# A hybrid decoder step with a dense expert stage: gate steps spread over the early up-projections, half of the expert selection one head later, the final norm by token blocks

## The chip, the core and the metric

The kernel runs on one core of a Trainium2 chip. The metric is the device time of one execution in microseconds, as the median of several runs; lower is better. The core has five engines with a queue of their own each: TensorE (PE, its weight loads are shown as PEld), VectorE (DVE), ScalarE (ACT), GpSimd (POOL) and SyncE (SP). An engine takes its queue strictly in order: an instruction that waits holds up all that stands behind it. Here SP only issues DMA transfers, and POOL almost only issues indirect DMAs, which gather rows from HBM by a list of numbers. All transfers share 16 DMA engines.

## What is computed

One inference step of one layer, for a prompt of 1024 tokens and 32 sample tokens (8 sequences of 4), at width 1024. The layer adds a token mixer (a gated delta rule and dilated windows), an attention to a memory of 256 entries, and PEER, a sparse expert layer; a last RMSNorm follows. The change is in PEER and in that norm, so these are the parts of the reference that matter:

```
def rmsnorm(x, g):
    xf = x.astype(F32)
    y = xf * lax.rsqrt(jnp.mean(xf * xf, axis=-1, keepdims=True) + NORM_EPS)
    return (y * g.astype(F32)).astype(x.dtype)

q = (xb @ w_pq).reshape(PEER_BLOCK, PEER_HEADS, 2, PEER_DHALF)      # 8 heads, two halves
s = jnp.einsum('thpc,hpnc->thpn', q, sub_keys)                      # 128 scores for each half
sv, si = lax.top_k(s, PEER_TOPK)                                    # best 16 of each half
cand = sv[:, :, 0, :, None] + sv[:, :, 1, None, :]
cv, ci = lax.top_k(cand.reshape(PEER_BLOCK, PEER_HEADS, 256), PEER_TOPK)
eid = i1 * PEER_NKEYS + i2                                          # i1, i2: taken from si by ci
gate = jax.nn.softmax(cv, axis=-1)
hid = jax.nn.gelu(jnp.einsum('thkd,td->thk', expert_u[eid], xb))
out = jnp.einsum('thk,thkd->td', gate * hid, expert_v[eid])
```

There are 16384 experts, and each token uses 8 heads x 16 = 128 of them.

## The kernel before

The prompt is cut into three groups of 384, 384 and 256 tokens (GROUPS); the 32 sample tokens go with the first (SG = 0, before and after the change). For each group `base` computes the mixer and the attention, and hands back `peer_route`, a generator that chooses the experts one head at a time. The chosen experts are then applied in one of two ways.

**By gathering** (`experts`, `experts_v`): 512 tokens of the first and third groups and the samples. For each of 128 slots POOL gathers the rows of expert_u that the tokens of a block want into a tile "gat" (128 x 1024, 4 buffers), DVE multiplies and sums them (L1282); after a GELU the same is done with expert_v, where DVE adds the row times its weight to the tile "acc" (L1431). That makes 1088 gathers of 512 KB. `paced` records them last of all, each behind an anchor instruction, and the scheduler that orders the finished program by its own estimates puts them wherever it finds room.

**Densely** (`dense`): the second group and the last 128 tokens of the third, 512 tokens (ND) together. All experts are computed for all tokens, in 128 slices of 128 experts, and a matrix of gates, zero almost everywhere, picks. Its parts, in the order of the program:

- The activations are loaded and split into a high and a low half ("C" and "B").
- 60 early up-projections (EARLY, chosen among the 128 slices): load a slice of expert_u ("wv", 2 buffers, L1347), split it on ACT and DVE ("wk", "zz"), 24 matmuls of 128x512, a GELU on ACT (L1355), and store the result to HBM (`uscr`, L1373). Between them stand the steps of `side`: the third group's `peer_route` (9 steps: one to begin, eight heads) and then `gate_extra`, 33 steps, of which 32 build the gates of four tokens each: DVE compares numbers (L1324, L1331), ACT does part of the comparing (L1330, L1333), four matmuls into "dl", and ACT copies the product into the halves "O" and "A" of the gate matrix (L1338). After each 8 of these steps SP stores both halves to `gscr` (L1341). PACE takes one step of `side` at every fourth early up-projection, 13 in all.
- What is left of `side` is run in one piece (`for _ in side`), then the tile "A" is taken again for the gates that are read back.
- The main loop, 128 slices (L1390 on): the gates of four slices are read back (`A<-gscr`, L1393), a slice of expert_v is loaded ("w", L1396) and split, the hidden values are multiplied by the gates (L1398), split, and multiplied by expert_v into eight sums in PSUM (tags "tp", "dl", "po", "ps"; the eighth goes through "vzs"). The 68 up-projections that were not early are computed between them.
- The eight sums are added to the residual "B" (L1423), and `finish_T` normalizes it: squares of all eight parts (L308), sums by matmul, a root on ACT (L321), a reciprocal, its spread over the partitions by matmul, eight multiplications (L328), then 32 transposes (L1467), eight copies (L1469) and eight stores (L1470).

`select` (called once or more for each head) takes the best 16 of the sums of both halves: DVE work on "tk" and "sel" that ends in the pair "ab" (L1242, L1243), a copy of the indices and one of "ab", spread 16-fold, on ACT (L1245, L1249, into "oh"), and DVE work that turns them into expert numbers (L1250 to L1256). In the first group it runs alone, in the second it is interleaved with `base` of the third group (`sprinkle`), and in the third with the early up-projections.

## Time and profile before

| | us |
|---|---|
| median of 3 runs | 4044.24 |
| these runs | 4036.69, 4044.24, 4068.52 |
| profiled execution, its own time | 4020.32 |
| its span, first to last instruction | 4018.5 |

| Stage, us of the span | what runs | TensorE busy | VectorE busy | DMA share |
|---|---|---|---|---|
| 772 to 905 | selection of the first group | 74% | 95% | 30% |
| 1530 to 2100 | base of the third group, selection of the second, gathers | 80% | 78% | 75% |
| 2394 to 2816 | early up-projections, selection of the third group, gathers | 98% | 86% | 95% |
| 2816 to 2889 | rest of the gate steps, gathers | 37% | 73% | 88% |
| 2889 to 3937 | main loop, gathers | 99% | 85% | 94% |
| 3937 to 3996 | end of the main loop | 100% | 51% | 31% |
| 3996 to 4018.5 | final norm and stores | 64% | 30% | 25% |

The profile is one execution; the sum of the prediction is made against its 4020.32 us, of which 1.8 us lie outside the span. It was 0.6% faster than the median of the runs shown. In its rows a line number is that of the kernel before, `out<-in` are the program's tile names, xN the number of instructions, and square brackets hold the idle time of the engine ahead of them and what ended it. The granted clock of TensorE (PEclk) is a share of 2.4 GHz.

### The profile page before, as it was taken

What the parts mean: (1) busy time and instruction counts of PE and PEld (TensorE: products, weight loads), DVE (VectorE), ACT (ScalarE), POOL (GpSimd) and SP (SyncE); (2) the same over time, 40 slices, a digit from 0 to 9 for tenths busy, and PEclk for the clock granted to TensorE, in tenths of its full rate; (3) what the DMA queues carried; (4) which work ended last, traced back from release to release, by engine and by line L of the source; (5) the groups of instructions that cost most, each with busy time, mean ns of one, the idle gap of its engine ahead of it and who ended that gap; (6) DMA issues with size and microseconds to landing.
All of it is one profiled execution on the core that took longest, in us unless ns stands there. A gap on an engine that the chain in (4) does not pass through costs nothing.

```text
span 4018.5 us, 53195 instructions
## 1 busy us (share of the span) xinstructions
PE 3533.0 (88%) x18135; PEld 2817.1 (70%) x18135; DVE 2889.7 (72%) x6660; ACT 1501.5 (37%) x3348; POOL 1358.8 (34%) x1255
## 2 busy tenths in 40 slices
PE   7998978968898787787887779999599999999999
PEld 6987865765676454456677657788477777787776
DVE  4334222599777766898669779997788888888885
ACT  5343413433233222123449652244533233333333
POOL 1000000001455554334333434444444444444441
PEclk9998878988999888887998889999799999999999
DMA  6443567423688888767768989999899999999994
GB/s 226 165 137 115 170 213 282 163 84 123 222 279 286 296 291 317 241 233 242 265 217 295 332 325 341 340 332 347 304 337 343 331 319 338 336 340 337 337 338 151
DMA packets 385600, 1074.23 MB, mean 267 GB/s; under 512 B 43280, under 2 KB 142160, under 8 KB 381232
## 3 DMA queue, kind: packets, MB, share of 16 engines
q0 software_dynamic: 159456, 580.58, 41.2%
q1 hardware_dynamic: 225872, 490.24, 34.9%
q8 instruction: 144, 2.36, 0.2%
q14 instruction: 128, 1.05, 0.1%
HBM read 995.22 MB, written 120.10 MB: 278 GB/s over the span
## 4 chain that ended last, share of the span: by engine, by line
PE 54%; DMA 13%; issue 12%; DVE 8%; POOL 7%; ACT 5%; POOLq 0%; SPq 0%; DVEq 0%; ACTq 0%
PE ps L150 36%; PE dl L150 10%; POOL gat L1273 7%; DMA gat<-expert_v,eid 5%; PE tp L150 4%; DMA gat<-expert_u,eid 3%; PE po L150 2%; DVE gat L1282 2%; DVE acc L1431 1%; ACT dtm L1330 1%; DMA w<-w_pq 1%; PE tp L870 1%; DMA zz<-ck 1%; DMA tmp<-tscr 0%; DVE dtm L1331 0%
## 5 line engine op out<-in xcount | busy, mean ns | idle before, releaser
L1273 POOL DMA_INDIRECT gat<-expert_u,eid x512 | 602.2, 1176 | 812.5 <-DVE hid L1282 482.4
L1273 POOL DMA_INDIRECT gat<-expert_v,eid x512 | 614.2, 1200 | 761.5 <-DVE acc L1431 566.0
L1431 DVE SCALAR_TENSOR_TENSOR acc<-gat,hid,acc 128x1024 f32<-128x1024 f32 x544 | 696.6, 1280 | 145.7 <-DMA gat<-expert_v,eid 138.6
L1282 DVE CUSTOM_DVE_ANT_0 gat<-gat,fr 128x1024 f32<-128x1024 f32 x544 | 660.0, 1219 | 137.2 <-DMA gat<-expert_u,eid 131.3
L150 PE MATMUL dl<-dtm,dtm 128*128 128x128 f32 (+2 forms) x2400 | 334.4, 290 | 62.0 <-ACT C L1338 20.6
L150 PEld LDWEIGHTS dl<-dtm,dtm 128*128 128x128 f32 (+1 forms) x2400 | 310.8, 203 | 84.4 <-ACT C L1338 23.5
L150 PE MATMUL ps<-C,w 128*128 128x384 f32 x768 | 283.6, 529 | 42.4 <-DMA w<-w_pq 32.3
L150 PE MATMUL dl<-O,dtm 128*128 128x512 f32 x1152 | 306.3, 396 | 0.0
L1291 ACT ACTIVATE dtm<-w 128x512 fp32r<-128x512 f32 x288 | 177.9, 628 | 300.7 <-PE dl L150 213.4
L150 PE MATMUL ps<-C,wk 128*128 128x512 f32 x1024 | 266.2, 402 | 24.8 <-ACT C L1291 17.0
L150 PE MATMUL ps<-C,zz 128*128 128x512 f32 (+1 forms) x1088 | 277.5, 391 | 0.0
L1291 ACT ACTIVATE wk<-wv 128x1024 fp32r<-128x1024 f32 x128 | 135.8, 1061 | 358.6 <-PE ps L150 304.8
L150 PEld LDWEIGHTS ps<-C,w 128*128 128x128 f32 x768 | 156.9, 209 | 151.0 <-DMA w<-w_pq 33.9
L150 PE MATMUL ps<-B,wk 128*128 128x512 f32 x1024 | 262.3, 398 | 0.0
L150 PEld LDWEIGHTS dl<-O,dtm 128*128 128x128 f32 x1152 | 217.2, 189 | 52.6
L150 PE MATMUL tp<-O,dtm 128*128 128x512 f32 x768 | 220.8, 403 | 31.3 <-ACT O L1291 30.5
L150 PEld LDWEIGHTS ps<-C,wk 128*128 128x128 f32 x1024 | 192.4, 191 | 74.9 <-ACT C L1291 18.9
L1292 DVE TENSOR_TENSOR dtm<-w,dtm 128x512 fp32r<-128x512 f32 x288 | 196.6, 685 | 66.1 <-issue 28.8
L150 PEld LDWEIGHTS ps<-C,zz 128*128 128x128 f32 x1088 | 204.3, 188 | 45.5
L150 PEld LDWEIGHTS ps<-B,wk 128*128 128x128 f32 x1024 | 194.4, 190 | 45.9
L150 PE MATMUL ps<-O,dtm 128*128 128x512 f32 x768 | 224.2, 396 | 0.0
L1292 DVE TENSOR_TENSOR zz<-wv,wk 128x1024 fp32r<-128x1024 f32 x128 | 156.5, 1223 | 74.2 <-ACT wk L1291 70.9
(500 smaller groups left out, 6346.4 us busy)
## 6 DMA issues: line engine op xcount, KB each, us to landing
wv<-expert_uT SPq DMA_DIRECT2D x128, 512.0 KB
w<-expert_v SPq DMA_DIRECT2D x128, 512.0 KB
w<-w_in SPq DMA_DIRECT2D x102, 512.0 KB
s_win<-cache_win SPq DMA_DIRECT2D x64, 512.0 KB
A<-gscr SPq DMA_DIRECT2D x32, 1024.0 KB
w<-w_pq SPq DMA_DIRECT2D x48, 512.0 KB
gscr<-C SPq DMA_DIRECT2D x12, 2048.0 KB
uscr<-tmp SPq DMA_DIRECT2D x60, 256.0 KB
```

Of the source, the lines that this page charges most:

```text
L150: x = self.nc.tensor.matmul(out, lhsT, rhs, **kw)
L870: nc.tensor.transpose(tp[:r, c, :], es[hh][:lq, j, o:o + r], C["ident"][:lq, :lq])
L1273: return self.nc.gpsimd.indirect_dma_start(out=dst, out_offset=None, in_=src, in_offset=bass.IndirectOffsetOnAxis(ap=idx, axis=0))
L1282: nc.vector.tensor_tensor_reduce(out=u, in0=u, in1=fr, scale=1.0, scalar=0.0, op0=ALU.mult, op1=ALU.add, accum_out=hid[:, s:s + 1])
L1291: nc.scalar.activation(hi, x, AF.Copy)
L1292: nc.vector.tensor_tensor(lo, x, hi.bitcast(F32), op=ALU.subtract)
L1330: nc.scalar.activation(o2[:, j], self.CB["iota"], AF.Abs, bias=i2[:, t:t + 1], scale=-1.0)
L1431: nc.vector.scalar_tensor_tensor(acc, v, c[:, s:s + 1], acc, op0=ALU.mult, op1=ALU.add)
```

## The change

There are four edits; SG and the groups are as before.

1. PACE is replaced by CLOSE and OPEN. The 41 steps of `side` are spread evenly over the first 50 early up-projections, the last stores follow at the 50th, and at the 56th the tile "A" is taken again and the first gates are read back (`load_gates(0)`). Nothing of `side` is left behind the early up-projections.
2. `select` becomes a generator in two halves. The second half, from the ACT copies on, is run a head later, after that head's top 16. "ab" gets a tag of its own ("sab", 3 buffers), "sel" has 5 buffers in place of 8.
3. `finish_T` works on blocks of 128 tokens: eight transposes into two PSUM tiles ("tp", "dl"), squares with their sum straight from PSUM on ACT, one addition, root and reciprocal, and two multiplications by root and gain straight from PSUM on DVE, each followed by its store. The gain is loaded as a row, spread over the partitions ("gf", in a "w" buffer).
4. `dense` returns the gain with the residual.

```
-PACE = (1, 1, 1, 1, 1, 1, 1, 1, 1, 1, 1, 1, 1)
+CLOSE, OPEN = 50, 56
@@ sel
-        return self.t(shape, "sel", 8, dt)
+        return self.t(shape, "sel", 5, dt)
@@ peer_route
+        late = []
         for h in range(8):
...
+            for x in late:
+                next(x, None)
+            late = []
             for b in range(0, nb, 2):
                 bs = slice(b, min(b + 2, nb))
-                self.select(P, sv[:, bs], si[:, bs], eid[:, h, bs], gate[:, bs, h])
+                late.append(self.select(P, sv[:, bs], si[:, bs], eid[:, h, bs], gate[:, bs, h]))
...
+            for x in late:
+                next(x)
+        for x in late:
+            next(x, None)
@@ select
-        ab = self.sel((P, 2, 2, 16), I32)[:m, :nb]
+        ab = self.t((P, 2, 2, 16), "sab", 3, I32)[:m, :nb]
         nc.vector.tensor_scalar(ab[:, :, 0], f, 4, None, op0=ALU.logical_shift_right)
         nc.vector.tensor_scalar(ab[:, :, 1], f, 15, None, op0=ALU.bitwise_and)
+        yield
         sf = self.sel((P, 2, 2, 16), BF16)[:m, :nb]
@@ dense
+        def load_gates(e):
+            nc.sync.dma_start(gs[e // GI % 2].rearrange("p s i t -> p s (i t)"),
+                              self.gscr[:, :, e * UT:(e + GI) * UT].rearrange("s p u -> p s u"))
+
         early = {e: i for i, e in enumerate(e for e in range(P) if e * EARLY // P != (e + 1) * EARLY // P)}
+        steps = 9 + EX // 4
         for e, i in early.items():
-            for _ in range(PACE[i // 4] if i % 4 == 0 and i // 4 < len(PACE) else 0):
-                next(side, None)
+            for _ in range((i + 1) * steps // CLOSE - i * steps // CLOSE if i < CLOSE else 0):
+                next(side)
+            if i == CLOSE:
+                for _ in side:
+                    pass
+            if i == OPEN:
+                gs = self.t((P, 2, ND // UT, GI, UT), "A", 1)
+                gs = [gs[:, j] for j in range(2)]
+                load_gates(0)
             nc.sync.dma_start(self.uscr[i], self.expert_up(e, fh, fl))
-        for _ in side:
-            pass
         self.rate = RATES[3]
-        gs = self.t((P, 2, ND // UT, GI, UT), "A", 1)
-        gs = [gs[:, j] for j in range(2)]
...
         h = self.t((P, KD, ND), "B", 1)
         nc.sync.dma_start(h, self.tscr[1])
+        gf = self.t((P, D), "w", WB)
+        nc.sync.dma_start(gf, I["g_final"].to_broadcast([P, D]))
@@ finish_T
-        self.norm_T(self.ks(h), 4, ND, self.ks(h))
-        for b in range(L // P):
-            self.rows(h, b * P, P, self.O["y_p"], t0 + b * P)
-        if EX:
-            self.rows(h, N1, EX, self.O["y_p"], SEQ - EX)
+        parts = [(c0, P, O["y_p"][t0 + c0:t0 + c0 + P]) for c0 in range(0, L, P)]
+        parts.append((N1, EX, O["y_p"][SEQ - EX:]))
+        for c0, m, out in parts:
+            qs = [self.p((P, 4, P), tag) for tag in ("tp", "dl")]
+            ss, y = self.small((P, 2)), [self.tmp() for _ in range(2)]
+            for i, q in enumerate(qs):
+                for k in range(4):
+                    nc.tensor.transpose(q[:m, k], h[:, 4 * i + k, c0:c0 + m], C["ident"])
+                nc.scalar.activation(y[i][:m], q[:m], AF.Square, accum_out=ss[:m, i:i + 1])
+            r = self.small((P, 1))
+            nc.vector.tensor_tensor(r[:m], ss[:m, :1], ss[:m, 1:], op=ALU.add)
+            nc.scalar.activation(r[:m], r[:m], AF.Sqrt, scale=1.0 / D, bias=C["eps"][:m, :1])
+            nc.vector.reciprocal(r[:m], r[:m])
+            for i, q in enumerate(qs):
+                z = y[i].rearrange("p a b -> p (a b)")
+                nc.vector.scalar_tensor_tensor(z[:m], q[:m].rearrange("p a b -> p (a b)"), r[:m], gf[:m, i * 512:(i + 1) * 512], op0=ALU.mult, op1=ALU.mult)
+                nc.sync.dma_start(out[:, i * 512:(i + 1) * 512], z[:m])
```

What this does to the order of the finished program is shown at three places. The first is TensorE among the early up-projections. An up-projection is three rows ("wk" twice, "zz" once); a head of the third group's selection is the four rows with "w" (w_pq) and "sk". Before, from one head on:

```order
L150 MATMUL ps_17561<-A_11016,w_17552 128x256 x8
L150 MATMUL ps_17571<-sk_17556,tmp_17560 128x128 x2
L150 MATMUL ps_17589<-A_11016,w_17554 128x256 x8
L150 MATMUL ps_17599<-sk_17556,tmp_17588 128x128 x2
L150 MATMUL ps_17660<-C_16428,wk_17656 128x512 x8
L150 MATMUL ps_17660<-B_16427,wk_17656 128x512 x8
L150 MATMUL ps_17660<-C_16428,zz_17657 128x512 x8
L150 MATMUL ps_17694<-C_16428,wk_17690 128x512 x8
```

Now, from one head on:

```order
L150 MATMUL ps_17107<-A_11016,w_17098 128x256 x8
L150 MATMUL ps_17117<-sk_17102,tmp_17106 128x128 x2
L150 MATMUL ps_17135<-A_11016,w_17100 128x256 x8
L150 MATMUL ps_17145<-sk_17102,tmp_17134 128x128 x2
L150 MATMUL ps_17206<-C_16428,wk_17202 128x512 x8
L150 MATMUL ps_17206<-B_16427,wk_17202 128x512 x8
L150 MATMUL ps_17206<-C_16428,zz_17203 128x512 x8
L150 MATMUL ps_17243<-A_11016,w_17234 128x256 x8
```

Before, three more up-projections followed before the next head; now the next head follows after one. All eight heads lie within nine up-projections, where they took up 32.

The second place is SP around the stores of the gates. The "A" that is read back is the one that the main loop needs first. Before, from the second pair of stores on:

```order
L1341 DMA gscr<-O_19489 128x2048
L1341 DMA gscr<-A_19490 128x2048
L1341 DMA gscr<-O_19629 128x2048
L1341 DMA gscr<-A_19630 128x2048
L1396 DMA w_20130<-expert_v 128x1024
L1341 DMA gscr<-O_19769 128x2048
L1341 DMA gscr<-A_19770 128x2048
L1396 DMA w_20175<-expert_v 128x1024
L1393 DMA A_19909<-gscr 128x16x128 x2
```

Now, from the last pair of stores on:

```order
L1350 DMA gscr<-O_19123 128x2048
L1350 DMA gscr<-A_19124 128x2048
L1356 DMA wv_19637<-expert_uT 128x1024
L1413 DMA w_20175<-expert_v 128x1024
L1395 DMA uscr<-tmp_19564 128x512
L1356 DMA wv_19671<-expert_uT 128x1024
L1395 DMA uscr<-tmp_19600 128x512
L1380 DMA A_19773<-gscr 128x16x128 x2
L1395 DMA uscr<-tmp_19634 128x512
```

The loads and stores of up-projections stand between the last stores of gates and their reading; before, the stores of three parts and the reading stood nearly side by side, behind all early up-projections.

The third place is DVE at the end of the main loop, from the next-to-last split of expert_v on ("dtm"), up to the additions to "B". Before:

```order
L1292 TENSOR_TENSOR dtm_27142<-w_27136,dtm_27141 128x512
L1419 TENSOR_TENSOR vzs_16429<-vzs_16429,ps_27077 128x512
L1292 TENSOR_TENSOR O_19910<-tmp_27069,O_19910 128x512
L1292 TENSOR_TENSOR dtm_27146<-w_27136,dtm_27145 128x512
L1292 TENSOR_TENSOR O_19910<-tmp_27113,O_19910 128x512
L1423 TENSOR_TENSOR B_27178<-B_27178,tp_19911 128x512
```

Now:

```order
L1301 TENSOR_TENSOR dtm_27142<-w_27136,dtm_27141 128x512
L1450 SCALAR_TENSOR_TENSOR acc_29867<-gat_30625,hid_29869,acc_29867 128x1024
L1436 TENSOR_TENSOR vzs_16429<-vzs_16429,ps_27077 128x512
L1301 TENSOR_TENSOR O_19911<-tmp_27069,O_19911 128x512
L1301 TENSOR_TENSOR dtm_27146<-w_27136,dtm_27145 128x512
L1450 SCALAR_TENSOR_TENSOR acc_29867<-gat_30628,hid_29869,acc_29867 128x1024
L1415 TENSOR_TENSOR tmp_27113<-tmp_27113,A_19773 128x512
L1450 SCALAR_TENSOR_TENSOR acc_29867<-gat_30631,hid_29869,acc_29867 128x1024
L1301 TENSOR_TENSOR O_19911<-tmp_27113,O_19911 128x512
L1450 SCALAR_TENSOR_TENSOR acc_29867<-gat_30634,hid_29869,acc_29867 128x1024
L1450 SCALAR_TENSOR_TENSOR acc_29867<-gat_30637,hid_29869,acc_29867 128x1024
L1442 TENSOR_TENSOR B_27178<-B_27178,tp_19912 128x512
```

The sums over gathered rows now go on up to the additions: 23 of them stand behind the last split of an up-projection ("zz"), where 2 stood before. Over the whole program their number is the same, 1088; from the first to the 63rd split of an up-projection there are 190 of them where there were 188, the piece of gate steps behind it, which held 32, is gone, and the main loop holds them as densely as before, about six for each up-projection.

## Rows read from the trace of the kernel before

**Rows 1.** Stretches: length, busy PE, PEld, DVE, ACT, POOL (instructions), clock, DMA share, GB/s
```profile
2394.00:2889.00 495.00, 440.14 (x2019) 362.38 (x2019) 416.90 (x1046) 203.23 (x374) 219.27 (x188) 0.95 0.94 337
...
2816.00:2889.00 73.00, 26.73 (x168) 25.14 (x168) 53.36 (x102) 44.75 (x113) 26.65 (x23) 0.69 0.88 309
...
3937.00:3996.00 59.00, 58.94 (x256) 46.16 (x254) 29.94 (x44) 19.84 (x31) 2.27 (x3) 1.00 0.31 116
```

**Rows 2.** Timeline of TensorE, rest of the gate steps: start, duration, [idle <-releaser]
```profile
2808.54 1.05 PE L150 MATMUL dl<-dtm,dtm 128*128 128x128 f32 x8
...
2855.13 7.42 PE L150 MATMUL dl<-dtm,dtm 128*128 128x128 f32 x40 [7.76 <-ACT A L1338]
2889.38 1.22 PE L150 MATMUL tp<-O,dtm 128*128 128x512 f32 x2 [26.83 <-ACT O L1291]
```

**Rows 3.** Timeline of SP there: last stores of gates, first reading
```profile
2864.54 0.64 SPq L1341 DMA_DIRECT2D gscr<-A  x1
...
2877.30 5.35 SPq L1393 DMA_DIRECT2D A<-gscr  x2
```

**Rows 4.** Waits, 2806 to 2900: us in total, times, longest
```profile
PE tp L150 <- ACT O L1291: 26.8, 1, 26.8
...
PE dl L150 <- ACT A L1338: 18.7, 5, 7.8
```

**Rows 5.** Stretches: four up-projections and a head; up-projections alone
```profile
2480.00:2511.50 31.50, 30.56 (x136) 24.84 (x136) 29.26 (x93) 9.15 (x14) 13.73 (x13) 1.00 0.94 346
...
2700.00:2740.00 40.00, 40.00 (x176) 32.54 (x175) 29.82 (x47) 12.88 (x17) 22.85 (x20) 1.00 0.99 362
```

**Rows 6.** The same stretch, L1282 on DVE alone
```profile
2480.00:2511.50 31.50, 14.66 (x24) 1.00 0.94 346
```

**Rows 7.** Groups, 2394 to 2890: busy us, mean ns | idle before <-releasers
```profile
L1292 DVE TENSOR_TENSOR zz<-wv,wk 128x1024 fp32r<-128x1024 f32 x61 | 74.6, 1223 | 23.5 <-ACT wk L1291 23.4
...
L1291 ACT ACTIVATE wk<-wv 128x1024 fp32r<-128x1024 f32 x61 | 64.7, 1060 | 162.7 <-PE ps L150 113.9 <-DMA wv<-expert_uT 26.3 <-DVE hid L1282 7.2
...
L1330 ACT ACTIVATE dtm<-cb,i 128x128 f32<-128x128 bf16 x96 | 30.0, 397 | 0.0
L1338 ACT ACTIVATE A<-dl 128x256 f32<-128x256 f32 x32 | 20.0, 666 | 0.0
L1338 ACT ACTIVATE O<-dl 128x256 f32<-128x256 f32 x32 | 19.1, 640 | 4.8 <-PE dl L150 4.8
L1333 ACT ACTIVATE dtm<-dtm 128x512 f32<-128x512 f32 x24 | 14.6, 634 | 0.0
```

**Rows 8.** Stretches, the gathers on POOL alone (xN)
```profile
2889.00:3937.00 1048.00, 474.47 (x391) 1.00 0.94 334
3937.00:3996.00 59.00, 1.15 (x1) 1.00 0.31 116
```

**Rows 9.** The spread copy of the selection on ACT: idle before it, who waited
```profile
  DVE sel L1243: 104.3, 28
...
  DVE oh L1250: 8.9, 8
```

**Rows 10.** Stretch: the first group's selection
```profile
772.00:905.00 133.00, 98.24 (x519) 85.27 (x518) 125.69 (x738) 48.99 (x107) 4.62 (x5) 0.91 0.30 98
```

**Rows 11.** Timeline, the final norm
```profile
3996.53 0.68 DVE L1423 TENSOR_TENSOR B<-B,ps 128x512 f32<-128x512 f32 x1
...
4000.19 1.28 ACT L321 ACT_TABLE_LOAD   x1
...
4001.49 0.26 ACT L321 ACTIVATE small<-ps,cf 128x4 f32<-128x4 f32 x1
4001.79 0.18 DVE L322 RECIPROCAL small<-small 128x4 f32<-128x4 f32 x1 [4.58 <-ACT small L321]
...
4003.28 5.35 DVE L328 SCALAR_TENSOR_TENSOR B<-B,gains,ps 128x512 f32<-128x512 f32 x8 [1.31 <-PE ps L150]
...
4014.78 0.60 ACT L1469 ACTIVATE tmp<-ps 128x512 f32<-128x512 f32 x1 [0.35 <-PE ps L1467]
```

More of the change, by code (lines that the diff above doesn't have):

```diff
@@ L1213, in peer_route @@
                 self.store_rows(hres, gi, self.hscr)
+            for x in late:
+                next(x, None)
+            late = []
             for b in range(0, nb, 2):
                 bs = slice(b, min(b + 2, nb))
-                self.select(P, sv[:, bs], si[:, bs], eid[:, h, bs], gate[:, bs, h])
+                late.append(self.select(P, sv[:, bs], si[:, bs], eid[:, h, bs], gate[:, bs, h]))
             if gi == SG:
-                self.select(NS, sv[:NS, nb:nb + 1], si[:NS, nb:nb + 1], eid[:NS, h, nb:nb + 1], gate[:NS, nb:nb + 1, h])
+                late.append(self.select(NS, sv[:NS, nb:nb + 1], si[:NS, nb:nb + 1], eid[:NS, h, nb:nb + 1], gate[:NS, nb:nb + 1, h]))
+            for x in late:
+                next(x)
+        for x in late:
+            next(x, None)
         for b, (m, c0) in enumerate(blocks):
@@ L1390, in dense @@
         for e in range(P):
-            if e % GI == 0:
-                g = gs[e // GI % 2]
-                nc.sync.dma_start(g.rearrange("p s i t -> p s (i t)"),
-                                  self.gscr[:, :, e * UT:(e + GI) * UT].rearrange("s p u -> p s u"))
+            g = gs[e // GI % 2]
+            if e % GI == 0 and e:
+                load_gates(e)
             v = self.t((P, KD, P), "w", WB)
@@ L1445, in finish, with finish_T @@
         nc.gpsimd.dma_start(out, acc)
-    def finish_T(self, h):
+    def finish_T(self, h, gf):
+        nc, C, O = self.nc, self.C, self.O
         t0, L = GROUPS[1]
-        self.norm_T(self.ks(h), 4, ND, self.ks(h))
-        for b in range(L // P):
-            self.rows(h, b * P, P, self.O["y_p"], t0 + b * P)
-        if EX:
-            self.rows(h, N1, EX, self.O["y_p"], SEQ - EX)
+        parts = [(c0, P, O["y_p"][t0 + c0:t0 + c0 + P]) for c0 in range(0, L, P)]
[15 more added lines that the diff above has]
+                nc.sync.dma_start(out[:, i * 512:(i + 1) * 512], z[:m])
     def store_rows(self, src, gi, scr):
@@ L1592, in run @@
                 self.sprinkle(1000)
-                self.finish_T(self.dense(route))
+                self.finish_T(*self.dense(route))
                 break
```

2 lines of the change are left out of this document (1 added, 1 removed).

## The prediction

> **What bounds the kernel now.** I read the stretches first. Ahead of the main loop TensorE is busy for 440.1 of 495 us, and its idle time is nearly all in one piece: from 2816 to 2889 it works 26.7 of 73 us, at a granted clock of 0.69 (that is the lower of its levels, 1.2 GHz, for much of the stretch; it had waited before) [rows 1]. The timeline shows why. This is the rest of the gate steps, which come after the last early up-projection: TensorE waits for ACT's copies between short bursts (7.76 us before the last), and then 26.83 us for the first operand of the main loop [rows 2]. That last wait is made on SP's queue: the last store of gates is issued at 2864.54 and the first reading of gates, which must see it landed, at 2877.30 [rows 3]; the rest is the reading itself. The waits of the stretch say the same: 26.8 us for ACT's "O", 18.7 us for the copies [rows 4]. In the main loop no such gap is left: its gathers run at 2.68 us each (1048 us / 391) with the DMA engines at 334 GB/s, and they end 59 us before the loop does; in these 59 us one gather is issued and the DMA rate is 116 GB/s [rows 1, 8]. So TensorE sets the end, with the gathers a reserve of some 59 us behind it.
>
> **Term 1, the gate steps among the early up-projections.** Removed: TensorE's idle 495 - 440.1 = 54.9 us, and the low clock. The 168 gate matmul records of the gap took 26.7 us; at the full-clock row, 1.05 us for 8 [rows 2], they would take 22.0. The floor ahead of the main loop is then 440.1 - 4.7 = 435.4 us, and 59.6 us can be gained at most.
>
> Against that stands what now lies in one place. By the order, the eight heads lie in nine up-projections, and DVE has there 9 splits, 49 gathered rows and 278 of the 378 selection instructions. Prices: a split is 1.22 us [rows 7]; a gathered row is 14.66 / 12 = 1.22 us [rows 6]; a head is what is left of a stretch of four up-projections and one head, 29.26 - 14.66 - 4 x 1.22 = 9.7 us [rows 5, 6]. DVE: 9 x 1.22 + 49 x 1.22 + 278/378 x 8 x 9.7 = 128 us. TensorE: an up-projection is 24 of the 176 records of a stretch that holds little else, 40 x 24 / 176 = 5.45 us, and a head 30.56 - 4 x 5.45 = 8.8 us [rows 5], so 9 x 5.45 + 8 x 8.8 = 119 us. DVE is thus longer by 9 us, and TensorE, which needs each split, waits for it. If DVE keeps the idle time that it has now (31.5 - 29.26 = 2.2 us for each head), it is 27 us. I take 10, nearer the lower end, because DVE has work queued from several sources there.
>
> Next, 19 of the 32 gate steps lie in seven up-projections. On ACT a step is (30.0 + 20.0 + 19.1 + 14.6) / 32 = 2.6 us [rows 7], and an up-projection 1.06 for the split and 0.63 for the GELU, at the price of L1333's shape [rows 7]: 19 x 2.6 + 7 x 1.69 = 61 us, against TensorE's 7 x 5.45 + 19 x 1.05 = 58. That costs 3 us. The halves "O" and "A" have one buffer each, so a part's first copy waits until the last part's store has landed, up to 12.8 us [rows 3], with the up-projections' ACT work queued behind it. Of the three such places two have several up-projections between, and one has about one; I take 2 us, bounds 0 and 38. On SP the wait before reading the gates back now has five issues of up-projections ahead of it; behind it stand up-projection loads that are two slices early. I cost it at nothing; without that cover it is 12.8 us. All of it: 59.6 - 10 - 3 - 2, about **-45 us** (-60 to 0).
>
> Do the transfers fit? The 495 us move 337 x 0.495 = 167 MB. Of these 30 gathers of 0.524 MB leave (32 of the gap go, the rest has 2 more), so 151 MB are left for 435 to 450 us, 336 to 347 GB/s. A 40 us stretch at 362 GB/s had TensorE busy all through [rows 5]. It fits, with little to spare.
>
> **Term 2, the second half of the selection a head later.** ACT's spread copies wait 104.3 us for DVE, 28 times, and hold up what stands behind them [rows 9]. In the first group this gives little: DVE is busy for 125.7 of 133 us [rows 10], so at most 7.3 us. The second group's selection runs within the base of the third, where no engine is near full and the trace does not show how much of a wait reaches the end; I allow the same again. DVE's 8.9 us of waiting for these copies [rows 9] may grow. I take **-3 us**, bounds -15 and +60 (the upper one is a rival below).
>
> **Term 3, the final norm.** Now: 21.3 us from the last addition's end (3997.2) to the end of the span (4018.5), and 3.1 of these behind the last copy [rows 11]. By blocks: the last four transposes, at the price of four gate matmuls, 1.05 [rows 2]; a square of the same shape as the copy, 0.60; root and reciprocal, 0.26 and 0.18, an addition like the latter; two multiplications of 5.35 / 8 = 0.67 [rows 11]. That is 3.6, with handovers 4.5 us for the first block. Of the later ones TensorE needs 2.1 each and waits for freed PSUM tiles, so 2.5: 4.5 + 7.5 + 3.1 = 15.1. **-6 us**, bounds -10 and 0.
>
> On ACT the new order has 71 table loads where it had 68. In the trace a load takes 1.28 us and the root follows 1.30 us after its start [rows 11], so three more are 3.9 us of an engine that does not set the end; I count nothing. The Trainium skill (ScalarE: Activation LUTs, "What ACT_TABLE_LOAD costs") gives 1.28 us and a drain of 1.38 on top for a switch. By it the three would be 8 us, and the sum, were all of them on the path, 8 us higher; the row here shows the load without the drain.
>
> **Term 4, the gathers at the end.** 21 more rows now stand behind the last up-projection's split. In 59 us that is 2.8 us each, against 2.68 in the loop, and 21 x 0.524 + 116 x 0.059 = 17.9 MB, 303 GB/s, below the loop's 334 [rows 1, 8]. But the additions to "B" now stand behind the last gathered row on DVE, and the squares behind the square of "acc" and a table load on ACT. **+2 us**, bounds 0 and +8.
>
> **Sum.** -45 - 3 - 6 + 2 = -52, from 4020.3 to 3968.3 us for an execution like the profiled one. The median shown is 4044.24 / 4020.32 = 1.006 times that execution; so I forecast **3992 us**.
>
> **Rivals.** *DVE bounds the packed heads.* The 27 us above in place of 10: -35 in sum, 3985, as a median 4009. For it: DVE is at 93% there now [rows 5]. Against it: its gathered rows are only loosely placed.
>
> *The transfers bound the packed stretch.* If it runs only at the 309 GB/s of the present gap [rows 1], where gate stores and gathers mix as they now will, 151 MB take 489 us and 6 of the 59.6 us are left: -13 in sum, 4007, as a median 4031. Against it: 362 GB/s was reached, and in the gap DVE and ACT held the gathers back.
>
> *DVE waits for ACT in turn (slower).* The late copy stands in ACT's queue behind work of the base that waits for TensorE, and DVE behind the copy. If each of the second group's 16 selections costs DVE the 3.7 us that ACT waits now (104.3 / 28), that is 60 us: +8 in sum, 4028, as a median 4053. It decides from 3.3 us each on, and is slower by over 1% from 5.8. Against it: that wait is now 8.9 / 8 = 1.1 us.
>
> *All covers hold.* DVE and ACT overlap as their sums allow and the first two selections give 15: -59.6 - 15 - 8 = -83, 3938, as a median 3961.
>
> **Chances.** The forecast 0.52 (its own range 3972 to 4010), DVE 0.18, transfers 0.12, the reversed wait 0.06, all covers 0.12. For the range I reach to the best case's 3961 with a little room, and above to the transfers' 4031: 3955 to 4040. One per cent, about what a measurement of this kernel can tell from no change, is 40 us: faster means under 4004. That holds for the best case, for most of the forecast (0.45) and a quarter of the DVE case: 0.62. Slower by over 1% needs the reversed wait at its worst, or a cost that I don't see: 0.05. The rest, 0.33, is the same.
>
> **What would show it.** Between the last early up-projection and the main loop TensorE's gap is gone and its clock stays at 1.0; from the start of the early up-projections to the main loop's first matmul it is about 450 us in place of 495. In the packed heads DVE is near 100% and TensorE shows short waits for splits. ACT's wait for L1243's successor is gone from the first two selections, with DVE's wait for the copy still small. The gathers' last issue lies within 10 us of the loop's end. From the last addition to the end there are about 15 us. I am wrong if the early part is not shorter than 475 us, if the main loop's TensorE falls under 98% because gathers come late, or if the base of the third group gets longer.

## The result, and the profile after

The changed kernel takes 3998.3 us (median of 4 runs, 3989.8 to 4007.5) against 4041.7 us (4 runs, 4036.7 to 4068.5, one more than those shown ahead): a ratio of 0.988, interval 0.983 to 0.993, a gain of 43 us. The gain is clear of none; whether it is more than one per cent the interval leaves open. Measured once more beside the experiments it is 0.9885 (0.9857 to 0.9913), 39 us between the medians.

One thing must be known before the traces are compared. The profiled execution of before took 4020.3 us, 21 us less than the median of its runs; that of after took 3995.9, 2 us less than its own. The two traces are thus only 24.4 us apart (4018.5 and 3994.1), and so I compare stretch by stretch. The stretches of the changed kernel (columns as in [rows 1]; the last two rows of this fence are the main loop and the end behind its last multiplication):

```profile
2405.33:2864.03 458.70, 438.01 (x2019) 360.07 (x2020) 386.70 (x1026) 202.11 (x372) 213.25 (x168) 0.98 0.94 339
2430.00:2590.00 160.00, 146.75 (x646) 119.00 (x645) 149.75 (x540) 41.47 (x68) 70.81 (x59) 0.98 0.89 314
2590.00:2790.00 200.00, 200.00 (x999) 167.65 (x998) 171.43 (x366) 132.44 (x267) 96.91 (x74) 1.00 0.96 349
2790.00:2864.00 74.00, 68.01 (x281) 54.45 (x280) 43.55 (x37) 19.72 (x24) 32.14 (x24) 0.95 0.98 352
2864.03:3978.04 1114.01, 1098.84 (x4659) 871.60 (x4658) 940.53 (x1224) 349.65 (x529) 504.41 (x421) 1.00 0.94 330
3978.04:3994.10 16.06, 5.46 (x32) 4.32 (x30) 10.43 (x23) 6.10 (x20) 0.56 (x1) 0.66 0.43 163
```

The early part, from the first store of an early result to the main loop's first matmul, is 458.7 us long where it was 495 [rows 1]. The gap ahead of the main loop is gone: from 2590 to 2790 us, where most gate steps now lie, TensorE is busy all the time at a granted clock of 1.00. The main loop takes 1114.0 us in place of 1106.0 (its last matmul ended at 3995.4 us before), and the end 16.1 in place of 23.1. That is -36.3 + 8.0 - 7.0 = -35.3 us. The dense part starts 11 us later than in the trace of before (2405.3 and 2394.4), which leaves some 24; whether the change did that is a question for the experiments.

What is left of TensorE's idle time in the early part (waits: us in total, times, longest; the third row ends as the stretch begins):

```profile
PE ps L150 <- ACT tmp L1204: 14.7, 16, 3.9
PE ps L150 <- ACT wk L1300: 6.0, 2, 4.4
PE ps L150 <- ACT tmp L1364: 5.1, 1, 5.1
```

14.7 + 6.0 is all of 458.7 - 438.0 = 20.7 us. L1204 is ACT's copy of a query of a head. In the packed heads it is late for a reason that the timeline shows (start, duration, [idle <-releaser]):

```profile
2483.19 1.06 ACT L1258 ACTIVATE oh<-sab 128x1024 bf16<-128x1024 int32 x1 [4.66 <-DVE sab L1251]
2484.15 0.36 ACT L1204 ACTIVATE tmp<-ps 128x256 f32<-128x256 f32 x1
...
2484.57 1.18 PE L150 MATMUL ps<-sk,tmp 128*128 128x128 f32 x4 [3.01 <-ACT tmp L1204]
```

The selection's spread copy stands ahead of the query copy on ACT and waits 4.66 us for DVE; TensorE pays 3.01 us for it. At 2514.7 us the same costs 3.9. The ordinary wait for such a copy is 0.47 us, and there are two in each head.

The other 6.0 us are two waits for a split. Around them lie the last stores and the first reading of gates on SP (SP, ACT and PE in order of time):

```profile
2783.92 0.37 SPq L1350 DMA_DIRECT2D gscr<-A  x1
...
2789.36 0.43 SPq L1356 DMA_DIRECT2D wv<-expert_uT  x1
2794.52 0.33 SPq L1395 DMA_DIRECT2D uscr<-tmp  x1
2794.95 8.53 SPq L1380 DMA_DIRECT2D A<-gscr  x2
...
2799.43 0.60 ACT L1364 ACTIVATE tmp<-ps 128x512 f32<-128x512 f32 x1 [4.93 <-PE ps L150]
2799.92 1.05 ACT L1300 ACTIVATE wk<-wv 128x1024 fp32r<-128x1024 f32 x1
2801.02 2.13 PE L150 MATMUL ps<-C,wk 128*128 128x512 f32 x8 [1.63 <-ACT wk L1300]
...
2803.54 3.28 SPq L1395 DMA_DIRECT2D uscr<-tmp  x1
2806.92 0.38 SPq L1356 DMA_DIRECT2D wv<-expert_uT  x1
...
2815.68 1.06 ACT L1300 ACTIVATE wk<-wv 128x1024 fp32r<-128x1024 f32 x1 [2.62 <-DMA wv<-expert_uT]
...
2816.79 3.78 PE L150 MATMUL ps<-C,wk 128*128 128x512 f32 x8 [4.36 <-ACT wk L1300]
2820.37 3.04 PE L150 MATMUL ps<-B,wk 128*128 128x512 f32 x8
2823.24 1.99 PE L150 MATMUL ps<-C,zz 128*128 128x512 f32 x8
```

The issue of the first reading of gates itself holds SP for 8.53 us, and the store behind it takes 3.28. Two loads of up-projections are therefore 17.6 us apart (2789.36 and 2806.92), ACT waits for the later slice until 2815.68, and TensorE waits 4.36 us for ACT. A wait for the last store of gates costs nothing here: the store of an up-projection ahead of the reading keeps SP until 2794.85, and the reading is issued 0.1 us later.

Nor is all of the 6.0 us due to that load. At 2801.02 no slice is late: ACT takes the split right behind the GELU of the slice before, with no wait between them, and the 1.63 us of TensorE are the time of these two. In the run with spread steps alone (below) both waits are such, though there too the reading holds SP, for 11 us:

```profile
PE ps L150 <- ACT wk L1291: 3.3, 2, 1.6
```

What the late load costs in waiting is thus 4.36 - 1.63 = 2.7 us in this trace. Behind that wait TensorE's next two groups take 3.78 and 3.04 us in place of some 2.0, at a granted clock of 0.53 from 2816.79 to 2823 us; from 2790 to 2864 us it is 0.95 in the mean.

The end of the main loop, and the norm:

```profile
3962.89 1.28 DVE L1450 SCALAR_TENSOR_TENSOR acc<-gat,hid,acc 128x1024 f32<-128x1024 f32 x1 [5.70 <-DMA gat<-expert_v,eid]
3964.09 0.69 DVE L1415 TENSOR_TENSOR tmp<-tmp,A 128x512 f32<-128x512 f32 x1
...
3965.55 0.73 PE L150 MATMUL tp<-O,dtm 128*128 128x512 f32 x2 [1.70 <-ACT O L1300]
...
3967.44 0.94 POOL L1282 DMA_INDIRECT gat<-expert_v,eid  x1 [1.86 <-DVE acc L1450]
...
3976.29 1.28 ACT L1461 ACT_TABLE_LOAD   x1
3977.58 0.30 ACT L1461 ACTIVATE fs<-fs,cf 128x1 f32<-128x1 f32 x1
...
3979.85 0.68 DVE L1442 TENSOR_TENSOR B<-B,ps 128x512 f32<-128x512 f32 x1
```

Gathers now go on to 10.6 us ahead of the loop's last matmul, where they ended 58 us ahead of it [rows 8]. A gathered row that came late held DVE for 5.70 us, the multiplication by gates stood behind it, and TensorE idled 1.70 us. But most of the main loop's extra time lies elsewhere. TensorE idles for 15.2 us of it, where it was 6.8. In the last 40 us of the loop its waits are 3.0 us; from 3289 to 3334 us they are 6.3. There the gathers change from the samples' rows to those of the third group:

```profile
3305.74 0.54 POOL L1464 DMA_DIRECT2D y_s<-acc  x1 [1.70 <-DVE acc L1463]
...
3315.11 1.23 DVE L1291 CUSTOM_DVE_ANT_0 gat<-gat,fr 128x1024 f32<-128x1024 f32 x1 [4.49 <-DMA gat<-expert_u,eid]
3316.26 0.69 DVE L1415 TENSOR_TENSOR tmp<-tmp,A 128x512 f32<-128x512 f32 x1
...
3317.73 1.22 PE L150 MATMUL tp<-O,dtm 128*128 128x512 f32 x2 [3.61 <-ACT O L1300]
```

The chain is the same, a late row on DVE with the multiplication by gates behind it. In the kernel before the samples' rows end at 3275 us, and TensorE has no such wait near there; why it has one now was not traced.

From the last addition (3980.5) to the end there are 13.6 us where there were 21.3 [rows 11].

### The profile page after: what moved, and what is told of

The parts are those of the page before. It is cut to its first block, busy times and chain, and to the rows that moved or that the text cites. A ratio compares the mean times of both kernels' runs of the same rounds, so it can differ in the third digit from the quotient of the medians.

```text
span 3994.1 us, 53131 instructions
## 1 busy us (share of the span) xinstructions
PE 3528.0 (88%) x18103; PEld 2820.1 (71%) x18103; DVE 2883.9 (72%) x6667; ACT 1500.9 (38%) x3353; POOL 1378.2 (35%) x1255
## 3 DMA queue, kind: packets, MB, share of 16 engines
q1 hardware_dynamic: 226016, 490.76, 35.3%
## 4 chain that ended last, share of the span: by engine, by line
PE 58%; DMA 14%; DVE 11%; issue 9%; ACT 4%; POOL 4%; SPq 0%; POOLq 0%; DVEq 0%; ACTq 0%
PE ps L150 37%; PE dl L150 11%; DMA gat<-expert_v,eid 6%; PE tp L150 5%; DMA gat<-expert_u,eid 5%; POOL gat L1282 4%; PE po L150 3%; DVE gat L1291 2%; DVE acc L1450 1%; DVE dtm L1340 1%; DMA w<-w_pq 1%; PE tp L870 1%; DVE tk L1180 1%; ACT dtm L1339 1%; ACT C L1347 0%
## 5 line engine op out<-in xcount | busy, mean ns | idle before, releaser
L1282 POOL DMA_INDIRECT gat<-expert_u,eid x512 | 622.3, 1215 | 798.3 <-DVE hid L1291 504.1
L1282 POOL DMA_INDIRECT gat<-expert_v,eid x512 | 613.6, 1199 | 764.1 <-DVE acc L1450 588.2
```

The lines of the kernel that those rows point to most:

```text
L1282: return self.nc.gpsimd.indirect_dma_start(out=dst, out_offset=None, in_=src, in_offset=bass.IndirectOffsetOnAxis(ap=idx, axis=0))
```

## The experiments

Each was measured beside the kernel before on the same chip; ratios are to it, and runs from different groups of measurements are compared by them. The stretches are read from each run's timeline: the start of the dense part (the first store of an early result), the early part, the main loop, the end behind its last matmul. "Rows" are gathers ahead of the dense part / in the early part / behind it (one on an edge can count twice), and the last column says how long ahead of the loop's last matmul the last one is issued.

| kernel | median us | ratio, interval | dense from | early | loop | end | sum of three | rows | last gather |
|---|---|---|---|---|---|---|---|---|---|
| before | 4043 | 1 | 2394 | 495 | 1106 | 23 | 1624 | 516/182/392 | 58 |
| changed | 3998 | 0.988, 0.983 to 0.993 | 2405 | 459 | 1114 | 16 | 1589 | 515/162/412 | 11 |
| changed again | 4004 | 0.9885, 0.9857 to 0.9913 | 2425 | 457 | 1109 | 16 | 1581 | 515/162/412 | 11 |
| late half alone | 4033 | 0.9972, 0.9944 to 0.9999 | 2410 | 494 | 1106 | 23 | 1624 | 515/183/391 | 58 |
| norm alone | 4048 | 0.9997, 0.9969 to 1.0025 | 2446 | 498 | 1103 | 17 | 1618 | 516/182/392 | 58 |
| spread alone | 4018 | 0.9925, 0.9895 to 0.9956 | 2422 | 455 | 1114 | 23 | 1592 | 516/160/414 | 23 |
| spread and norm | 4016 | 0.9924, 0.9894 to 0.9955 | 2410 | 456 | 1118 | 16 | 1591 | 515/160/414 | 23 |
| changed, half put back | 4051 | 1.0016, 0.9985 to 1.0047 | 2411 | 467 | 1123 | 35 | 1625 | 502/162/425 | -17 |
| small buffers alone | 4056 | 1.0006, 0.9969 to 1.0043 | 2400 | 499 | 1111 | 23 | 1633 | 502/186/402 | 37 |
| heads spaced | 3992 | 0.9878, 0.9843 to 0.9913 | 2398 | 450 | 1111 | 20 | 1581 | 516/160/414 | 2 |
| heads spaced, again | 3998 | 0.9866, 0.9820 to 0.9911 | 2405 | 451 | 1115 | 19 | 1585 | 516/160/414 | 2 |
| 3600 units | 4008 | 0.9912, 0.9882 to 0.9942 | 2411 | 469 | 1106 | 17 | 1592 | 527/163/400 | 35 |
| spaced, 3750 units | 3996 | 0.9859, 0.9809 to 0.9909 | 2410 | 460 | 1109 | 16 | 1585 | 519/163/406 | 22 |
| 32 rows left out | 3993 | 0.9862, 0.9801 to 0.9923 | 2398 | 460 | 1109 | 17 | 1586 | 515/162/380 | 87 |

**The parts alone, and one part undone.** First the changed kernel with the second half of the selection put back behind the first:

```diff
-            for x in late:
-                next(x, None)
             late = []
...
             for x in late:
-                next(x)
-        for x in late:
-            next(x, None)
+                for _ in x:
+                    pass
```

> The changed kernel with the second half of each selection put back right behind its first half, in all three groups; the spread gate steps and the norm by blocks stay, and so do the smaller buffers of the selection. Theory A (the late second half costs what the traces differ by ahead of the dense part: its start moved from 2394 to 2405 us): the dense part starts 11 us earlier again, near 2394, and the median is about 11 us under the changed kernel's 3998, so 3987, ratio to the kernel before 0.986. Rival B (the 11 us are a difference between two executions, and the late half is worth the forecast -3 us): start of the dense part near 2405 as often as 2394, median 4001.

It gave 4051 us: all of the gain was gone, which neither theory had. It did not go ahead of the dense part (2411 us) but behind its start: the early part is 8 us longer than in the changed kernel, the main loop 9 and the end 19. At the end gathers were still under way:

```profile
4017.95 0.94 POOL L1279 DMA_INDIRECT gat<-expert_v,eid  x1 [0.30 <-issue]
...
4025.47 1.28 DVE L1447 SCALAR_TENSOR_TENSOR acc<-gat,hid,acc 128x1024 f32<-128x1024 f32 x1 [0.69 <-DMA gat<-expert_v,eid]
...
4028.50 1.29 DVE L1460 SCALAR_TENSOR_TENSOR acc<-acc,fs,gat 128x1024 f32<-128x1024 f32 x1
```

The loop's last matmul ended at 4000.6. The last gather is issued 17 us later, and the end is 35 us in place of 16. The next three runs have each part of the change alone. The late half on the kernel before (with its buffers, five and three in place of eight):

```diff
-                self.select(P, sv[:, bs], si[:, bs], eid[:, h, bs], gate[:, bs, h])
+                late.append(self.select(P, sv[:, bs], si[:, bs], eid[:, h, bs], gate[:, bs, h]))
...
+            for x in late:
+                next(x)
...
         nc.vector.tensor_scalar(ab[:, :, 1], f, 15, None, op0=ALU.bitwise_and)
+        yield
```

> The kernel before with nothing but the late second half of the selection. Theory A: the dense part starts 11 us later than in the kernel before under the same conditions, median 4042 + 11 = 4053, ratio 1.003. Rival B (forecast): -3 us, 4039, ratio 0.999. The rival of the prediction in which DVE waits for ACT in each of the second group's 16 selections: +60 us, 4102.

4033 us: -11 between the medians, with an interval from -23 to 0. Theory A falls, and the reversed wait with it. Its three stretches are those of the kernel before (1624 us), so what it gains lies ahead of the dense part, where one trace each cannot show it (below). The norm alone, which is the change's new finish_T and the loading of its gains ahead of the additions:

```diff
+        gf = self.t((P, D), "w", WB)
+        nc.sync.dma_start(gf, I["g_final"].to_broadcast([P, D]))
...
-                self.finish_T(self.dense(route))
+                self.finish_T(*self.dense(route))
```

> The kernel before with nothing but the final norm by blocks. Forecast: from the last addition to the end 15.1 us in place of 21.3, -6 us. As the trace of the changed kernel has it: 13.6 us, -7.7 us, with median 4034, ratio 0.998. A rival: the new order of work at the end lies elsewhere in another program, and the end gets no shorter.

Its trace has the shorter end (16.9 us in place of 23.1), its median no difference beyond the interval of +-11 us. The spread gate steps alone, which is the change's loop over the early up-projections with load_gates:

```diff
-            for _ in range(PACE[i // 4] if i % 4 == 0 and i // 4 < len(PACE) else 0):
-                next(side, None)
+            for _ in range((i + 1) * steps // CLOSE - i * steps // CLOSE if i < CLOSE else 0):
+                next(side)
```

> The kernel before with nothing but the gate steps spread among the early up-projections and the first reading of gates moved ahead. Forecast: -45 us and +2 us for the gathers at the end, 3999, ratio 0.989. Theory A with the stretches of the changed kernel: the early part 36 us shorter, the main loop 7 us longer, -29 us, 4013, ratio 0.993. Were the part alone worth all of the median's 43 us, 3999.

4018 us, -30 by the ratio and -32 in the three stretches: theory A's size. The norm's trace settles the question of the 11 us. Its program is that of the kernel before, instruction for instruction on every engine, up to the main loop's end; yet its dense part starts at 2446 us, where that of before started at 2394. The stretch from 1270 us to that start in both:

```profile
1270.00:2394.38 1124.38, 881.93 (x4651) 667.62 (x4649) 860.89 (x2121) 464.99 (x1202) 469.61 (x423) 0.87 0.80 278
```

```profile
1270.00:2445.56 1175.56, 924.28 (x4674) 701.62 (x4672) 866.26 (x2128) 467.31 (x1204) 479.45 (x426) 0.84 0.77 268
```

The first is the kernel before, the second the norm alone. With one program TensorE's busy time differs by 42 us, at a mean granted clock of 0.87 and 0.84, and the stretch by 51. A difference of 11 us there, from one trace each, says nothing.

**What took the gain away.** The run with the half put back kept the smaller buffers. Two runs part the causes: the changed kernel with the selection of before, eight buffers included (the first expectation below), and the kernel before with nothing but the smaller buffers (the diff, and the second):

```diff
-        return self.t(shape, "sel", 8, dt)
+        return self.t(shape, "sel", 5, dt)
...
-        ab = self.sel((P, 2, 2, 16), I32)[:m, :nb]
+        ab = self.t((P, 2, 2, 16), "sab", 3, I32)[:m, :nb]
```

> The changed kernel without anything of the late selection: its second half right behind the first, and the buffers of before (eight in one pool, in place of five and three). Theory C (the parts add up: spread gate steps -25 us, norm by blocks -6, and what cost the run with the second half put back its gain is the smaller buffers): 4043 - 25 - 6 = 4011, gathers' last issue before the loop's end. Rival D (the immediate selection itself takes the gain away when gate steps are spread and the norm goes by blocks): 4050, with gathers issued for 20 us behind the loop, as in that run.

> The kernel before with nothing but the selection's buffers cut from eight to five and three, its second half right behind the first. With them, the spread gate steps and the norm by blocks gave 4051; with the eight buffers 4016. Theory E (the cut moves some 11 gathered rows from ahead of the dense part to behind it, which costs only where no reserve of gathers is left): here the reserve of 59 us takes 11 rows x 2.7 = 30 us, and the time stays, 4043 (within 8 us). Rival F (the cut makes DVE wait in the selections and lengthens the base itself): 4043 + 34 = 4077.

With eight buffers: 4016 us, theory C's size, and rival D is out. Within some 12 us the parts add up; the norm's 6 us are below that. The buffers alone on the kernel before: 1.0006 (-13 to +17 us), so rival F's +34 is out. The table's rows speak for theory E: with the small buffers and the half not late, 502 gathers lie ahead of the dense part, in both programs, and 515 or 516 in every other of like pace (501 and 515 if each counts once, by its start). With the half late the same buffers leave them at 515. Counted at the same matmuls of TensorE, the rows fall behind from the base of the third group on: 2 or 3 are missing at 1.9 ms of the span, 12 or 13 at 2.3 ms. At 2.68 us each [rows 8] these 14 rows are 38 us, and the three stretches are 1625 - 1591 = 34 us longer where the gate steps are spread. On the kernel before the last gather moves from 58 to 37 us ahead of the loop's end, and the stretches grow by 9. That the rows alone make up the 34 us is not shown: 11 us of them are in the early part, where TensorE has one wait of 10.9 us for a split, behind the reading of gates. Why the scheduler puts these rows later was not traced further.

**The changed kernel again**, with no edit:

> The changed kernel once more, as the measure for what stands beside it. Median 3998, ratio 0.989. If the place at which the dense part starts is a matter of the execution (2394, 2422 and 2446 us so far with one program ahead of it), its start lies anywhere from 2394 to 2446 here too, and the three stretches behind it keep their lengths: 459, 1114 and 16 us.

Nearly as expected: dense part from 2425 us, and 457, 1109 and 16 us. The main loop differs by 5.5 us between two executions of one program.

**The packed heads.** The heads at every second early up-projection:

```diff
-            for _ in range((i + 1) * steps // CLOSE - i * steps // CLOSE if i < CLOSE else 0):
+            if i < CLOSE and (i % 2 == 0 or i >= 18):
                 next(side)
```

> The changed kernel with the eight heads of the third group at every second early up-projection, in place of one at each, and the 32 gate steps one by one behind them, closed at the same place. If DVE bounds the packed heads (the changed kernel's TensorE idles for 13 us from 2430 to 2590 us), these 13 us come back: early part 446 in place of 459, and the time 3998 - 13 = 3985 where the gathers let it. If the transfers bound what is behind the dense part's start, the early part gets shorter and the main loop longer by as much, 3998.

```profile
2398.03:2848.14 450.11, 434.47 (x2019) 356.24 (x2020) 385.13 (x1025) 202.93 (x372) 201.12 (x166) 0.99 0.95 343
2848.14:3958.86 1110.72, 1098.85 (x4659) 870.57 (x4658) 935.97 (x1220) 347.25 (x525) 511.27 (x422) 1.00 0.94 331
2410.00:2570.00 160.00, 151.42 (x683) 123.17 (x683) 156.15 (x581) 43.78 (x73) 70.38 (x62) 1.00 0.94 333
```

The early part is 450 us, 7 to 9 shorter, not 13. In 160 us of heads (the third row) TensorE now idles 8.6 us in place of 13.3, though DVE is at 98% there and was at 94%: DVE's load as a whole is not what sets the wait. At the end 4 us are given back: the last gather is issued 2 us ahead of the loop's last matmul, its additions lie among the norm's work on DVE, and the end takes 20 us. The time is 3992 us, not to be told from the changed kernel's.

A second run was to move the first reading of gates two slices later:

```diff
-CLOSE, OPEN = 50, 56
+CLOSE, OPEN = 50, 58
```

> The changed kernel with the heads at every second early up-projection, and the first reading of gates issued ahead of the 59th early up-projection in place of the 57th. In the changed kernel that reading stands on SP until the last store of gates has landed, with the loads of two up-projections behind it; TensorE then idles for 6.0 us (4.5 in the run with the spaced heads: 1.63 and 2.88). Two slices later the store has landed by itself, some 10 us more: theory G says these idle times go, the early part takes 445 us in place of 450, and the time is 3992 - 5 = 3987. Rival: the reading then ends so close to the main loop's start that the first multiplication by gates waits for it, and the main loop's first matmul shows a wait of several us; 3992 or more.

The scheduler placed the reading exactly where it had been; the order is the same on every engine. So this is the program with spaced heads a second time (early part 451, TensorE's waits for the slices 1.63 and 3.53 us), and theory G has not been tried. The traces leave it little room: of these waits 1.63 us each come without a late load, and in the changed kernel the reading does not stand waiting for the store.

**Where the gathers lie.** More of them in the base of the third group:

```diff
-RATES = (4000, 3900, 2000, 3700)
+RATES = (4000, 3600, 2000, 3700)
```

> The changed kernel with gathered rows placed more densely in the base of the third group (a row for each 3600 units of TensorE's work in place of 3900, some 20 rows more ahead of the dense part), as many as the removed gap used to hold. If the main loop's 7 us extra are rows that come late, it takes 1107 us in place of 1114 and the last gather is issued some 50 us ahead of its end; the time is 3998 - 7 = 3991 if the base takes these rows beside its work. Rival: the base gets longer by their DVE time, 20 x 1.25 = 25 us, and the time is 4016.

The main loop is 1106.4 us, as expected, and the last gather 35 us ahead of its end. But the early part is 469 us. There TensorE has one wait of 8.9 us for a split, at 2833 us and again behind the first reading of gates (on SP from 2808.77 to 2819.04), and another for a head's keys:

```profile
PE ps L150 <- ACT wk L1300: 8.9, 1, 8.9
PE ps L150 <- ACT tmp L1364: 5.9, 5, 2.7
PE ps L150 <- DMA sk<-sub_keys: 3.9, 1, 3.9
```

What the loop gains the early part gives back; the longest wait behind the reading goes from 1.6 to 10.9 us over the runs of the table, while two executions of one program differ by less than 1 us. With spaced heads and 3750 units it came out likewise:

```diff
-RATES = (4000, 3900, 2000, 3700)
+RATES = (4000, 3750, 2000, 3700)
```

> The changed kernel with the heads at every second early up-projection and some 10 rows more in the base of the third group (a row for each 3750 units in place of 3900). The heads alone gave 3992, with the last gather issued 2 us ahead of the main loop's end and an end of 19.8 us in place of 16. Ten rows earlier the gathers end 25 us sooner: main loop 1107 in place of 1111, end 16 in place of 20, so 3985. Rival: the early part gets longer by as much, as in the run with 3600 units (469 us), 4000.

460 us early, 1109 in the loop, 16 at the end: the rival's early part, the forecast's end, and a median as the changed kernel's. Last, 32 rows left out:

```diff
-        for s in range(c.shape[1]):
+        for s in range(c.shape[1] - cut):
...
-            yield from self.experts(fr, *sel[b], acc)
+            yield from self.experts(fr, *sel[b], acc, 32 if gi == 2 else 0)
```

> The changed kernel that leaves out 32 gathered rows of expert_v at the very end of the list (the last 32 of the last block's 128, with their additions). If the main loop's extra 2 to 8 us (1108 to 1114 us against 1104 to 1106) are rows that come late, it takes 1106 us here, the last gather is issued some 80 us ahead of its end, and the time is 3995 to 4000 against 4001. If the transfers as a whole bound what stands behind the dense part's start, 32 rows less are 32 x 2.7 = 86 us less to move and the time falls by well over 10 us, to 3980 or less.

The three stretches sum to 1586 us, between the changed kernel's two executions (1589 and 1581), though 32 rows less are moved. So the transfers as a whole do not bound the changed kernel. The main loop is 1109 us, as in one of these two. In its last 40 us TensorE no longer waits (3.0 and 1.9 us in the two executions of the changed kernel), but at the samples' end it does as before, for 5.1 us (6.3 and 3.9). So the rows at the very end cost the loop 2 to 3 us; why the rows at the samples' end come late stays open.

## Why the prediction was right, and where its steps were off

The forecast was 3992 us and -52; measured are 3998 and -43, and the case that came is the forecast's own. But the agreement is closer than the working deserves, and in part luck. By the sum an execution like the profiled one was to take 3968 us; the profiled one of after took 3996. The factor of 1.006 from the profiled execution to the median, taken over from before, belongs to that one execution alone: for after it is 1.001. Behind the dense part's start I had -45 - 6 + 2 = -49; the two traces of the changed kernel give -35 and -43.

**Term 1** (-45): the early part fell by 36 us (38 in the second execution). The floor of 435.4 was right: TensorE is busy for 438.0. Of the 23 us lost to it, where I had 15:

- Packed heads, 10: the waits for the heads' copies are 14.7 us, of which 16 x 0.47 = 7.5 would be there in any case (they stand in the 54.9 idle us that I counted as removed: 7.1 before). The price was near, the way was not. I had TensorE wait for its splits, and in the trace it waits for ACT's query copies, which stand behind the spread copy, which waits for DVE. Spaced heads gave back 7 to 9 us of the early part.
- Gate steps on ACT, 3, and the halves' stores, 2: nothing. From 2590 to 2790 TensorE is busy all through. My ACT sum of 61 us against 58 lay in work that runs ahead.
- SP's wait for the gates, 0: this was the step that failed. I had priced the wait for the store (12.8 us without cover), which costs nothing here, and not the issue of the reading, 8.5 us of SP, although [rows 3] has it with 5.35. The loads "two slices early" were cover for less than the 17.6 us by which two of them came apart. It cost 2.7 us of waiting (1.9 in the second execution), and most of the 2.6 us of busy time above the floor would be the slower groups behind it. The other 3.3 us are two splits that stand right behind a GELU on ACT; I had no term for them.

**Term 2** (-3): alone -11, interval -23 to 0; with the others 0.9885 against 0.9924, in the same direction. The forecast lies inside. ACT's waits for the selection's copy went as I had it for the first group, and not for the second. In the kernel before, from 772 to 910 and from 1580 to 1860 us:

```profile
ACT oh L1249 <- DVE sel L1243: 28.5, 9, 8.0
...
ACT oh L1249 <- DVE sel L1243: 39.6, 8, 13.9
ACT oh L1249 <- DVE tk L1180: 12.5, 2, 7.6
```

In the changed kernel, the same two stretches:

```profile
ACT oh L1258 <- DVE sel L1264: 6.5, 6, 1.9
ACT oh L1258 <- DVE sab L1251: 2.3, 3, 0.9
...
ACT oh L1258 <- DVE sel L1264: 26.5, 5, 9.8
ACT oh L1258 <- DVE sab L1251: 24.7, 5, 8.6
ACT sel L1254 <- DVE cv L1265: 10.2, 4, 3.9
```

In the first group 28.5 us became 8.8 (6.5 + 2.3). DVE is still busy there for 125 of 133 us, and the group's last copy comes 3 us earlier (995.1 in place of 998.3). In the second 52 us became 61, of which 24.7 are still a wait for the pair; 26.5 have a new reason: there is one "oh" tile, so the second of two late copies waits until DVE has read the first (L1264). That the buffers are a part of the edit with a price of its own, 34 us where the half is not late and no reserve is left, I had not seen at all.

**Term 3** (-6): the end fell by 7.0 us, and from the last addition by 7.7. ACT's table load stands in the tail with 1.28 us, and the root starts 1.29 us after the load's start, as in [rows 11]. The Trainium skill (ScalarE: Activation LUTs, "What ACT_TABLE_LOAD costs") puts a drain of 1.38 us on top of a switch; the rows of this case show none, with 0.02 us between the instruction ahead and the load, and 0.01 between the load and the root.

**Term 4** (+2, 0 to +8): +8.0 and +2.5 in two executions. The way was right, work of the loop behind late rows on DVE, and so was the last issue, 10.6 us ahead of the loop's end. The place was right for a part only: 3.0 and 1.9 us of TensorE's waits lie in the last 40 us, and 6.3 and 3.9 at the end of the samples' rows, which I had not looked at.

**The rivals.** *DVE bounds the packed heads*: the early part's 36 us lie midway between the forecast's 45 and this rival's 28, but not for its reason. The heads' waits above the usual are 7 us, not 27, with DVE at 94% from 2430 to 2590 us. *Transfers bound the packed stretch*: no; the early part ran at 339 GB/s, and leaving rows out changes no sum. *DVE waits for ACT in turn*: no; the late half alone is no slower, and DVE's waits for the spread copies fell from 8.9 us [rows 9] to 4.0. *All covers hold*: no. What I had not among them is what the runs showed as the real edge: the 59 us reserve of gathers is spent, and a program with 14 rows later in the order loses the whole gain.

**The signs** that I had named. As forecast: the gap is gone, the main loop's TensorE is busy for 98.6%, the last issue lies 10.6 us ahead of its end for 10, and the norm takes 13.6 us for 15. Near: 459 us for 450. Not as forecast: the clock is 1.00 from 2590 to 2790 us but 0.95 behind that, DVE is at 94% in the heads, TensorE's waits there are for query copies and not for splits, and ACT's wait for the pair is nearly gone from the first group (2.3 us) but not from the second (24.7). One was badly chosen. "The base of the third group gets longer" was to show me wrong; the dense part starts 11 and 30 us later in two executions of the changed kernel, and one program ahead of it varies by 51.

## What to carry to other kernels

A stage that is shortened spends the reserve of whatever runs beside it: count what is left (here 58 us of gathers, then 11), because the next edit that moves a few rows of it costs in full. Compare two traces stretch by stretch and only where the program is known to vary little; a stretch at a changing granted clock needs several executions. When tiles are given smaller buffers to make room for an edit, that is an edit with its own price, and an undoing of the edit that keeps them measures something else.

## What the runs showed of the hardware

One program took 1124 and 1176 us from 1270 us to the dense part's start in two executions, at mean granted clocks of 0.87 and 0.84, TensorE's busy time differing by 42 us for the same work. Behind that start, in the main loop, TensorE is busy for 98% or more and the granted clock is 0.99 or 1.00 in the mean of every run. From the dense part's start to the end two executions of one program agree within 8 us (two pairs).

In the changed kernel the issue of one reading of gates (2 MB from HBM, 4096 pieces of 512 bytes) held SP for 8.5 us, in the nine other runs that have it among the up-projections for 8.0 to 12.4, and the next load of a slice stood behind it. From 2803 to 2808 us, when only this reading's data moved, the rate was 289 GB/s, where it was 400 from 2795 to 2803.

The 68 and 71 table loads of ACT in the two kernels took 1.28 us each, in the median 0.02 us behind the instruction ahead and 0.01 us ahead of the next.
